# A hybrid attention and state-space decoder block: both value halves in one PSUM bank, another clock behind the order of all queues, and TensorE's order in attention taken from the source

## The chip, the core and the metric

The kernel runs on one core of one Trainium2 chip. The metric is the device time of one execution in microseconds (us); lower is better. The core has five engines with a queue each: TensorE (PE in the profile, its weight loads PEld), VectorE (DVE), ScalarE (ACT), GpSimd (POOL) and SyncE (SP, which here issues nearly all DMAs).

## What is computed

The reference is one decoder layer on x of 2048 tokens by 1024 channels, in float32. Cut to what matters here:

```
h = rmsnorm(x);  P = h @ W_in      # q, k, v, z_a, indexer q/k/w, z_b, x/B/C, dt, gates
A = attention(q, k, v) over the 256 keys that the indexer scores highest, 8 heads, 2 KV heads of 64
A = A * silu(z_a)
B = Mamba-2 scan (conv, 16 heads, chunks of 128), group norm with silu(z_b)
m = sigmoid(gA) * (A @ W_pa) + sigmoid(gB) * (B @ W_pb)
out = rmsnorm(x + m @ W_out)
```

## The kernel before

Products that need float32 accuracy are made of float16 halves: a value is split into a high half and a low half (the rest), and three products are added in PSUM. The tokens are 16 tiles of 128. The kernel runs in stages that overlap at their edges: the scan branch with its projections (to about 700 us of the profiled span), the indexer's scores, the search for the 256th score and the other projections (to about 1400), and attention together with the final products (from about 1400 to the end). Names below are those of the source.

**Attention.** For each query tile i (a block), `att_A(i)` loads q, splits it, transposes it by DMA into Q1, makes all scores once (L1398, tile `lq`) and lets VectorE take each row's maximum (L1401, `jk`, `mxs`). The maxima go as two extra columns into `q2t`, which a DMA transposes into Q2. `att_B(i)` then walks over the two KV heads g and the key tiles j <= i. One step makes the scores of four heads (L1495 with Q1, L1497 with Q2, tile `lg`), VectorE adds the mask (L1504), ScalarE takes the exponential (L1505) and its float16 high half `ph` (L1509), GpSimd the low half `pl` (L1512). The step's products with the values come three steps later (`LAG`), in `pv` for `ph` (L1431) and later still in `pv_lo` for `pl` (L1440). The value tile `Vt` holds, for each key, 64 high halves, a column of ones (it gives the sum of the exponentials) and 64 low halves: 129 columns. `pv` multiplies `ph` with all 129, `pv_lo` multiplies `pl` with the first 65. The result of two heads takes one PSUM bank, so four heads take two tiles of the pool `psO`, which has two: a group's first `pv` waits until the last group has been read out.

After a group's last step VectorE reads each bank out: reciprocal of the sums (L1447), copy of the high part (L1453), addition of the low part (L1454); GpSimd multiplies by the reciprocal (L1455). After both groups, `tail(i)` multiplies by silu(z_a) on VectorE (L1463, 128x512), and norm, split and a DMA transpose give `oT`.

**Final products.** `fin_M(i)` multiplies `oT` with W_pa (L1536 to L1538) and the scan's result with W_pb (L1543 to L1545), gates the two (L1548 to L1550), and splits and transposes into `mT`. `fin_O(i)` multiplies with W_out (L1574 to L1576) and adds x.

**What sets the order.** The source is a set of Python generators that `interleave` weaves: inside block i, the steps of `att_B(i)` are the main line, `att_A(i+1)` and the final products of earlier tiles are spread between them by fixed estimates. Block 0 and 1 and `att_A(2)` are woven with the last projections in `early_att`, ahead of `attention`. What is written in this order is then put in order once more when the program is built: a scheduler runs through a model of the machine, and whenever an engine is free by the model's clock, it takes for it the instruction written earliest among those whose inputs the model has ready. That fixes each engine's queue; the chip runs each queue strictly in that order. So an instruction that the model thinks late is overtaken by later ones, and one that it thinks ready stands where it is written, whatever the chip will find. In the profiled run TensorE's order from 750 to 1350 us is exactly that of the source; in the attention it departs from it by a few instructions here and by up to a hundred there; VectorE's departs from it everywhere.

Of the kernel before, what the change touches and what calls it, by code (L numbers as in the profile page):

```python
# [9 lines left out]
FT = mybir.dt.float32  # L10
# [5 lines left out]
AF = mybir.ActivationFunctionType  # L16
OP = mybir.AluOpType
# [4 lines left out]
P = 128  # L22
# [6 lines left out]
HD = 64  # L29
# [11 lines left out]
def MARK(label):  # L41
    pass


def _chain(*gens):
    for g in gens:
        yield from g


def _run_all(gen):  # L50
    while True:
        try:
            next(gen)
        except StopIteration as e:
            return e.value
# [10 lines left out]
def _pace(gen, t):  # L66

    while t > 0:
        try:
            w = next(gen)  # L70
        except StopIteration:
            return
        if w is None:
            return
        t -= w
        yield w
# [23 lines left out]
def interleave(main, sides):  # L100

    total = max(1e-9, main[1])
    done, pos = 0.0, [0.0] * len(sides)
    for w in main[0]:
        done += w
        for k, (gen, ln) in enumerate(sides):
            while pos[k] is not None and pos[k] < ln * done / total:
                try:
                    pos[k] += next(gen)
                except StopIteration:  # L110
                    pos[k] = None
    for k, (gen, ln) in enumerate(sides):
        if pos[k] is not None:
            for _ in gen:
                pass
# [32 lines left out]
XO = 0  # L148
# [9 lines left out]
def hybrid_block(ctx, tc, a, out, dbg=None):  # L158
    nc = tc.nc
    V, A, PL, PE, SP = nc.vector, nc.scalar, nc.gpsimd, nc.tensor, nc.sync  # L160

    def pool(name, bufs, **kw):
        return ctx.enter_context(tc.tile_pool(name=name, bufs=bufs, **kw))
# [510 lines left out]
    def scan(u):  # L674
# [89 lines left out]
        for k in range(4):  # L764
# [12 lines left out]
            elif u < 15:  # L777
                scan_load(u + 1, k - 2)
            yield 1
        TAIL.append(tail())  # L780

    def need(key):
# [357 lines left out]
    Vt = kv.tile([P, NT, G, 130], F16, name="Vt")  # L1140
# [178 lines left out]
    psO = pool("psO", 2, space=PSUM, reuse_waits="tile")  # L1319
# [10 lines left out]
    def rowscale(f2, name, pool_):  # L1330

        t = pool_.tile([P, 1], I32, name=name + "t", tag="rs1")
        s = pool_.tile([P, 1], I32, name=name + "s", tag=name + "s")
        v = pool_.tile([P, 1], I32, name=name + "v", tag=name + "v")
        V.tensor_scalar(t, f2.bitcast(I32), 1, 0x3F800000, OP.logical_shift_right, OP.bitwise_and)
        V.tensor_scalar(s, t, -1.0, 204.0 * 2 ** 23, OP.mult, OP.add)
        V.tensor_scalar(v, t, 50.0 * 2 ** 23, None, OP.add)
        return s.bitcast(FT), v.bitcast(FT)

    def split_T(src, s, t, dst, nb, pe=False):  # L1340

        A.activation(t[:, 0], src, AF.Copy, scale=s)
        n = nb * P // (2 if nb == KC else 1)
        for c in range(0, nb * P, n):
            V.scalar_tensor_tensor(t[:, 1, c:c + n], src[:, c:c + n], s, t[:, 0, c:c + n], OP.mult, OP.subtract)
        yield SPY
        if not pe:
            SP.dma_start_transpose(dst.rearrange("p a k t -> p (a k) t"), t.rearrange("p a n -> p (a n)"))
            return
        m = KC // nb  # L1350
        for hl in range(0, 2, m):
            pp = lgps2([P, m, nb, P], F16)
            for a in range(m):
                for k in range(nb):
                    PE.transpose(pp[:, a, k], t[:, hl + a, k * P:(k + 1) * P], id16)
            A.copy(dst[:, hl:hl + m], pp)
            yield KC * 0.056
# [4 lines left out]
    def load_mt(i):  # L1362

        mts[i] = at.tile([P, NT, P], BF, name="mkt")
        SP.dma_start_transpose(mts[i][:, 0:i + 1], msk[i, :, 0:(i + 1) * P])
# [56 lines left out]
    def pv():  # L1422

        MARK("attB")
        if len(plo) >= (PLD if lag > 1 else 1):
            pv_lo()
        i, g, j, ph, pl, B = pend.pop(0)
        if j == 0:
            B["po"] = [psO.tile([P, 2, 256], FT, name="po", tag="po") for _ in range(2)]
        for h in range(4):  # L1430
            PE.matmul(B["po"][h // 2][:, h % 2, 0:129], ph[:, h], Vt[:, j, g, 0:129], start=(j == 0 and h % 2 == 0), stop=False)  # L1431
        plo.append((i, g, j, pl, B))
        while j == i and plo:
            pv_lo()

    def pv_lo():
        i, g, j, pl, B = plo.pop(0)
        po, oa = B["po"], B["oa"]
        for h in range(4):
            PE.matmul(po[h // 2][:, h % 2, 0:65], pl[:, h], Vt[:, j, g, 0:65], start=False, stop=(j == i and h % 2 == 1))  # L1440
        if j == i:
            rc = at.tile([P, 4], FT, name="rc")
            for b in range(2):
                pob = po[b]
                oag = oa[:, 4 * g + 2 * b:4 * g + 2 * b + 2]
                rcb = rc[:, 2 * b:2 * b + 2]
                V.reciprocal(rcb, pob[:, :, 64])  # L1447
                if XO == 2:
                    for h in range(2):
                        A.activation(oag[:, h], pob[:, h, 0:64], AF.Copy, scale=rcb[:, h:h + 1])  # L1450
                        V.scalar_tensor_tensor(oag[:, h], pob[:, h, 65:129], rcb[:, h:h + 1], oag[:, h], OP.mult, OP.add)
                else:
                    V.tensor_copy(oag, pob[:, :, 0:64])  # L1453
                    V.tensor_tensor(oag, oag, pob[:, :, 65:129], OP.add)  # L1454
                    (V if XO else PL).tensor_tensor(oag, oag, rcb[:, :, None].to_broadcast([P, 2, HD]), OP.mult)  # L1455
            if g == G - 1:
                tails.append(tail(i, B))

    def tail(i, B):

        MARK("attB")
        oaf = B["oa"].rearrange("p h d -> p (h d)")
        V.tensor_tensor(oaf, oaf, B["za"].rearrange("p h d -> p (h d)"), OP.mult)  # L1463
        t = at.tile([P, 2, H * HD], F16, name="spa", bufs=1)
        f2 = at.tile([P, 1], FT, name="f2a")
        A.activation(t[:, 1].bitcast(BF), oaf, AF.Square, accum_out=f2)
        s_a, v_a = rowscale(f2, "ra", at)
        va = ac.tile([P, 1], FT, name="va", bufs=NQ)
        V.tensor_tensor(va, v_a, ra, OP.mult)
        oT = ac.tile([P, 2, 4, P], F16, name="oT", bufs=NQ)  # L1470
        yield
        yield from split_T(oaf, s_a, t, oT, 4, i == NT - 1)
        oTs[i] = (oT, va)

    def flush():
        while pend:
            pv()
        while tails:
            _run_all(tails.pop(0))
# [121 lines left out]
    def last(i):  # L1601
        if i == NT - 1:
            flush()
        return
        yield

    def fin_stream(first):
        for i in range(NT):
            o = fin_O(i - 1, fi) if i else iter(())
            while i not in oTs:  # L1610
                yield None
            if i == NT - 1:
                yield from _take(o, 8)
            mg_ = fin_M(i, fi)
            if i == 0:
                lw = load_out() if first else iter(())
                for w in mg_:
                    yield w
                    next(lw, None)
            elif i < NT - 1:  # L1620
                yield from _take(mg_, MO)
                yield from _zip(mg_, o, ZM, 16)
            else:
                yield from mg_
                yield from o
        yield from fin_O(NT - 1, fi)
# [27 lines left out]
    def attention(first):  # L1654
        nonlocal fi, at, pw, lag
        lag = LAG
        with tc.tile_pool(name="fi", bufs=2, reuse_waits="tile") as fi, tc.tile_pool(name="at", bufs=2, reuse_waits="tile") as at, \
                tc.tile_pool(name="pw", bufs=3, reuse_waits="tile") as pw:
            if not first:
                _run_all(att_A(0))  # L1660
            i0 = NA if first else 0
            if first:
                load_mt(NA)
            fs = fin_stream(first)
            wt = [max(tB(i), T_MIN) for i in range(NT)]
            rate = (NT - 1) * T_FIN / sum(wt[i0:])
            for i in range(i0, NT):
                sides = [(_pace(fs, rate * wt[i]), rate * wt[i])]
                if i + 1 < NT:
                    sides.append((att_A(i + 1), A_F * tA(i + 1)))  # L1670
                interleave((_chain(att_B(i), last(i)), tB(i)), sides)
            for _ in fs:
                pass

    attention(True)


    def exact_topk(gp):
# [95 lines left out]
```

## Time and profile before

| | |
|---|---|
| time, median of 3 runs | 2226.74 us (2224.58 to 2228.22) |
| profiled execution | 2230.14 us, span 2228.4 us |
| TensorE busy | 2037.3 us (91%), mean granted clock 0.973 of 2.4 GHz |
| VectorE busy | 1803.7 us (81%) |
| ScalarE, GpSimd busy | 1126.2 us (51%), 841.2 us (38%) |

The span is the time from the first to the last instruction; 1.7 us lie around it. A busy TensorE counts a matmul from its start to its modelled end, and matmuls overlap, so a pause shorter than that overlap doesn't show as idle.

### The profile page before, as it was taken

What the parts mean: (1) busy time and instruction counts of PE and PEld (TensorE: products, weight loads), DVE (VectorE), ACT (ScalarE), POOL (GpSimd) and SP (SyncE); (2) the same over time, 40 slices, a digit from 0 to 9 for tenths busy, and PEclk for the clock granted to TensorE, in tenths of its full rate; (3) what the DMA queues carried; (4) which work ended last, traced back from release to release, by engine and by line L of the source; (5) the groups of instructions that cost most, each with busy time, mean ns of one, the idle gap of its engine ahead of it and who ended that gap; (6) DMA issues with size and microseconds to landing.
All of it is one profiled execution on the core that took longest, in us unless ns stands there. A gap on an engine that the chain in (4) does not pass through costs nothing. (4 is left out here: it accounts for less than half of the span.)

```text
span 2228.4 us, 43416 instructions
## 1 busy us (share of the span) xinstructions
PE 2037.3 (91%) x15537; PEld 1386.7 (62%) x15537; DVE 1803.7 (81%) x4954; ACT 1126.2 (51%) x1971; POOL 841.2 (38%) x1208
## 2 busy tenths in 40 slices
PE   6889999899998999989999899988989899999997
PEld 5656666566766878768877788634444444544553
DVE  8888888988888567888998887577889888887763
ACT  5444443433342267646746731245566566666671
POOL 4423335533435433310102124124455444544550
PEclk9999999999999999999999999999999999999998
DMA  4444322322222332342344435485454334234231
GB/s 144 131 105 112 94 66 84 108 76 62 67 61 84 95 94 80 87 128 90 115 142 134 126 118 172 107 213 125 106 116 108 100 97 102 81 89 96 62 91 45
DMA packets 371195, 229.06 MB, mean 103 GB/s; under 512 B 209996, under 2 KB 333720, under 8 KB 370968
## 3 DMA queue, kind: packets, MB, share of 16 engines
q1 hardware_dynamic: 370968, 226.19, 37.9%
q8 instruction: 124, 2.03, 0.4%
q14 instruction: 103, 0.84, 0.1%
HBM read 123.82 MB, written 53.90 MB: 80 GB/s over the span
## 5 line engine op out<-in xcount | busy, mean ns | idle before, releaser
L1512 POOL TENSOR_TENSOR pl<-p,ph 128x512 f16<-128x512 f32 x272 | 328.3, 1211 | 428.8 <-ACT ph L1509 407.1
L1505 ACT ACTIVATE p<-p,lnb,qsc 128x512 f32<-128x512 f32 x270 | 217.3, 811 | 194.1 <-DVE p L1504 193.6
L443 PEld LDWEIGHTS <-xh 128*128 128x128 f16 x2560 | 250.6, 99 | 48.0 <-issue 12.8
L442 PEld LDWEIGHTS <-xh 128*128 128x128 f16 x2560 | 252.0, 99 | 41.2 <-issue 5.9
L444 PEld LDWEIGHTS <-xl 128*128 128x128 f16 x2560 | 250.7, 99 | 32.5 <-issue 2.5
L1504 DVE TENSOR_TENSOR p<-lg,mkt 128x512 f32<-128x512 f32 x266 | 181.2, 684 | 53.9 <-PE lg L1497 49.9
L1401 DVE CUSTOM_DVE_ANT_0 jk<-lq,mka 128x512 bf16<-128x512 f32 (+3 forms) x304 | 187.6, 617 | 33.9 <-PE lq L1398 27.7
L1509 ACT CAST ph<-p 128x512 f16<-128x512 f32 x272 | 165.3, 614 | 6.1
L1087 ACT ACTIVATE jkS<-sca,XX 128x384 int8<-128x384 f32 (+3 forms) x104 | 138.6, 1333 | 53.6 <-DVE XX L1077 34.9
L1398 PE MATMUL lq<-KK,Q 128*128 128x512 f16 (+3 forms) x320 | 103.2, 350 | 21.0 <-DVE mxs L1401 16.4
L1431 PE MATMUL po<-Vt,ph 128*128 128x129 f16 x1088 | 113.7, 221 | 8.8 <-DVE oa L1454 3.4
L1089 DVE TENSOR_SCALAR_CACHE_REDUCE jkV<-sca,XX 128x1536 uint8<-128x1536 f32 (+4 forms) x78 | 111.8, 1434 | 2.6
L1497 PE MATMUL lg<-Q,KK 128*128 128x512 f16 x272 | 102.9, 382 | 12.0 <-DMA Q<-q2t 12.0
L1495 PE MATMUL lg<-Q,KK 128*128 128x512 f16 x272 | 103.8, 382 | 6.8 <-DVE p L1504 6.7
L1166 ACT ACTIVATE gt<-gt 128x512 f32<-128x512 f32 x64 | 40.1, 627 | 135.6 <-DVE gt L1165 135.1
L1574 PE MATMUL fi<-wo,mT 128*128 128x512 f16 x256 | 98.4, 384 | 9.8 <-DMA mT<-spm 5.7
L951 ACT ACTIVATE r<-acc 128x512 f32<-128x512 f32 (+3 forms) x152 | 79.3, 542 | 49.3 <-DVE sca L952 32.4
L1440 PEld LDWEIGHTS <-pl 128*128 128x128 f16 x1088 | 66.3, 98 | 58.3 <-issue 5.7
L1543 PE MATMUL fi<-wpb,obt 128*128 128x512 f16 x256 | 97.6, 381 | 4.4 <-DVE gtl L1548 2.8
L1575 PE MATMUL fi<-wo,mT 128*128 128x512 f16 x256 | 98.7, 386 | 0.0
L1576 PE MATMUL fi<-wo,mT 128*128 128x512 f16 x256 | 98.6, 386 | 0.0
L1545 PE MATMUL fi<-wpb,obt 128*128 128x512 f16 x256 | 97.8, 382 | 0.0
(802 smaller groups left out, 6454.4 us busy)
## 6 DMA issues: line engine op xcount, KB each, us to landing
bc<-acr SPq DMA_DIRECT2D x64, 256.0 KB, 3.2
gd<-gt SPq DMA_DIRECT2D x64, 256.0 KB, 2.5
gtl<-gd SPq DMA_DIRECT2D x32, 512.0 KB, 4.4
xt<-in_x SPq DMA_DIRECT2D x16, 512.0 KB, 4.3
e<-ecr SPq DMA_DIRECT2D x128, 64.0 KB, 3.1
obn<-ohl SPq DMA_DIRECT2D x64, 128.0 KB, 2.2
pst<-in_w_out SPq DMA_DIRECT2D x16, 512.0 KB, 4.4
xr<-in_x SPq DMA_DIRECT2D x32, 256.0 KB, 3.1
```

Source lines behind the costliest of these rows:

```text
L442: PE.matmul(ps, xh[:, c, tk], hi[:, c], start=(first and c == 0), stop=False)
L443: PE.matmul(ps, xh[:, c, tk], lo[:, c], start=False, stop=False)
L444: PE.matmul(ps, xl[:, c, tk], hi[:, c], start=False, stop=(last and c == KC - 1))
L1087: A.activation(jkA[:, :n], sct[i], AF.Sign, bias=thr[:, 0, k:k + 1], scale=-1.0, accum_out=cnt[:, 0, k:k + 1])
L1089: V.tensor_scalar(jkV[:, :n], sct[i], thr[:, 0, k:k + 1], 0.0, OP.is_lt, OP.add, accum_out=cnt[:, 0, k:k + 1])
L1401: V.tensor_tensor_reduce(jk[:, :c1 - c0], ps[:, :c1 - c0], mk[:, c0:c1], 1.0, -BIG, OP.add, OP.max, mxs_[:, h, c:c + 1])
L1431: PE.matmul(B["po"][h // 2][:, h % 2, 0:129], ph[:, h], Vt[:, j, g, 0:129], start=(j == 0 and h % 2 == 0), stop=False)
L1495: PE.matmul(ps, KHt[g][:, js], Q1[:, hs], start=True, stop=False)
L1504: V.tensor_tensor(p32, ps, mb, OP.add)
L1505: A.activation(p32, p32 if masked and not onP else ps, AF.Exp, bias=lnb, scale=qsc[g])
L1509: A.copy(ph, p32)
L1512: PL.tensor_tensor(pl, p32, ph, OP.subtract)
```

## The change

Three things are changed. First, the four heads of a group share one PSUM bank of 4 x 128 floats: `ph` is multiplied with the 65 columns of high halves and ones and, in a second matmul, with the 64 low halves, which add onto the same 64 columns. What was left to VectorE after the group (copy, addition) is now done by the accumulation; one reciprocal and one multiplication straight from PSUM remain, and the multiplication with silu(z_a) goes to GpSimd, once for each group. Second, the scheduler's clock is another, more detailed model of the machine (`schedule_with_timeline_sim`), for the whole program. Third, TensorE's instructions in `attention` (blocks 2 to 15 and all final products) are not put in order by the scheduler; they keep the order of the source.

```
         if j == 0:
-            B["po"] = [psO.tile([P, 2, 256], FT, name="po", tag="po") for _ in range(2)]
+            B["po"] = psO.tile([P, 4, 128], FT, name="po", tag="po")
         for h in range(4):
-            PE.matmul(B["po"][h // 2][:, h % 2, 0:129], ph[:, h], Vt[:, j, g, 0:129], start=(j == 0 and h % 2 == 0), stop=False)
+            PE.matmul(B["po"][:, h, 0:65], ph[:, h], Vt[:, j, g, 0:65], start=(j == 0 and h == 0), stop=False)
+            PE.matmul(B["po"][:, h, 0:64], ph[:, h], Vt[:, j, g, 65:129], start=False, stop=False)
...
         for h in range(4):
-            PE.matmul(po[h // 2][:, h % 2, 0:65], pl[:, h], Vt[:, j, g, 0:65], start=False, stop=(j == i and h % 2 == 1))
+            PE.matmul(po[:, h, 0:65], pl[:, h], Vt[:, j, g, 0:65], start=False, stop=(j == i and h == 3))
         if j == i:
             rc = at.tile([P, 4], FT, name="rc")
-            for b in range(2):
-                pob = po[b]
-                oag = oa[:, 4 * g + 2 * b:4 * g + 2 * b + 2]
-                rcb = rc[:, 2 * b:2 * b + 2]
-                V.reciprocal(rcb, pob[:, :, 64])
...
-                    V.tensor_copy(oag, pob[:, :, 0:64])
-                    V.tensor_tensor(oag, oag, pob[:, :, 65:129], OP.add)
-                    (V if XO else PL).tensor_tensor(oag, oag, rcb[:, :, None].to_broadcast([P, 2, HD]), OP.mult)
+            oag = oa[:, 4 * g:4 * g + 4]
+            V.reciprocal(rc, po[:, :, 64])
+            V.tensor_tensor(oag, po[:, :, 0:64], rc[:, :, None].to_broadcast([P, 4, HD]), OP.mult)
+            PL.tensor_tensor(oag, oag, B["za"][:, 4 * g:4 * g + 4], OP.mult)
...
         oaf = B["oa"].rearrange("p h d -> p (h d)")
-        V.tensor_tensor(oaf, oaf, B["za"].rearrange("p h d -> p (h d)"), OP.mult)
...
-    attention(True)
+    with tc.manual_schedule(engines={PE.engine}):
+        attention(True)
...
-    with tile.TileContext(nc) as tc:
+    with tile.TileContext(nc, schedule_with_timeline_sim=True) as tc:
```

## Rows read from the trace of the kernel before

**Rows 1.** The page: busy time of each engine, its share of the span, its instructions.

```profile
PE 2037.3 (91%) x15537; PEld 1386.7 (62%) x15537; DVE 1803.7 (81%) x4954; ACT 1126.2 (51%) x1971; POOL 841.2 (38%) x1208
```

**Rows 2.** Busy time in stretches: PE, PEld, DVE, ACT, POOL, granted clock, DMA.

```profile
0.00:1400.00 1400.00, 1290.96 (x10319) 994.32 (x10320) 1158.03 (x3233) 658.58 (x1211) 485.12 (x872) 0.97 0.36 103
...
1480.00:2229.00 749.00, 677.33 (x4724) 349.79 (x4722) 596.31 (x1563) 438.31 (x712) 337.35 (x314) 0.98 0.39 95
...
500.00:600.00 100.00, 99.59 (x666) 69.36 (x664) 84.37 (x214) 39.72 (x88) 40.03 (x58) 1.00 0.22 63
900.00:1000.00 100.00, 87.27 (x713) 71.59 (x712) 87.16 (x260) 55.40 (x104) 23.64 (x69) 0.93 0.41 112
```

**Rows 3.** TensorE's waits from 1400 us on: total us, times, longest.

```profile
PE lq L1398 <- DVE mxs L1401: 16.4, 27, 1.8
PE lg L1497 <- DMA Q<-q2t: 12.0, 9, 2.8
PE lg L1495 <- DVE p L1504: 6.7, 8, 2.0
...
PE po L1431 <- DVE oa L1454: 3.4, 7, 1.1
PE fi L1536 <- DVE gtl L1549: 3.3, 2, 1.8
PE fi L1574 <- DVE gtl L1548: 2.9, 2, 1.9
PE fi L1543 <- DVE gtl L1548: 2.8, 1, 2.8
...
PE po L1431 <- DVE rc L1447: 1.4, 1, 1.4
```

**Rows 4.** TensorE's waits before 1400 us: two small helper products.

```profile
PE trp L257 <- ACT jkS L251: 11.8, 3, 7.2
...
PE trp L992 <- DVE w_branch_ac L986: 4.9, 1, 4.9
```

**Rows 5.** TensorE's timeline: start, length (from first start to last end), line, count.

```profile
1975.25 0.39 PE L1431 MATMUL po<-Vt,ph 128*128 128x129 f16 x4
1975.47 0.38 PE L1574 MATMUL fi<-wo,mT 128*128 128x512 f16 x1
...
2143.29 0.41 PE L1440 MATMUL po<-Vt,pl 128*128 128x65 f16 x8
2143.53 0.38 PE L1536 MATMUL fi<-wpa,oT 128*128 128x512 f16 x1
```

**Rows 6.** Groups by line: count, busy us, mean ns; a weight load, the read-out, its nearest relatives.

```profile
L1440 PEld LDWEIGHTS <-pl 128*128 128x128 f16 x1088 | 66.3, 98 | 58.3 <-issue 5.7
...
L1447 DVE RECIPROCAL rc<-po 128x2 f32<-128x2 f32 x64 | 10.3, 160 | 9.6 <-PE po L1440 9.1 <-POOL oa L1455 0.5
L1454 DVE TENSOR_TENSOR oa<-oa,po 128x128 f32<-128x128 f32 x64 | 18.1, 283 | 0.5
L1453 DVE COPY oa<-po 128x128 f32<-128x128 f32 x64 | 17.7, 277 | 0.0
L1463 DVE TENSOR_TENSOR oa<-oa,za 128x512 f32<-128x512 f32 x16 | 16.3, 1021 | 8.0 <-POOL oa L1455 8.0
L704 DVE TENSOR_TENSOR xd<-trp,dts 128x256 f32<-128x256 f32 x64 | 26.5, 416 | 5.1 <-ACT xk L702 4.6
...
L1455 POOL TENSOR_TENSOR oa<-oa,rc 128x128 f32<-128x128 f32 x64 | 29.2, 463 | 19.4 <-DVE oa L1454 18.2
L734 POOL TENSOR_TENSOR zu<-xk,zu 128x256 f32<-128x256 f32 x64 | 53.5, 836 | 97.1 <-DVE xk L733 90.6 <-DVE hz L572 4.5 <-DVE ss L431 1.7
```

**Rows 7.** TensorE's timeline at the start of block 2.

```profile
1443.97 0.32 PE L1398 MATMUL lq<-KK,Q 128*128 128x384 f16 x1
1444.13 0.38 PE L1545 MATMUL fi<-wpb,obt 128*128 128x512 f16 x1
...
1450.65 0.59 PE L1497 MATMUL lg<-Q,KK 128*128 128x512 f16 x2 [0.96 <-DMA Q<-q2t]
```

## Prediction before the run

> **What bounds the kernel now.** I read the page first: TensorE is busy for 91% of the span, VectorE for 81% [rows 1]. Either could be the bound, so the stretches come next. Before 1400 us TensorE is busy for 1291.0 of 1400 us, from 1480 us on for 677.3 of 749 us, and VectorE for 596.3 of the same 749 [rows 2]. TensorE leads in both, with 109 us idle in the first and 72 us in the second, and VectorE is close behind in attention. The reader is to see also how far two stretches lie apart: TensorE is 99.6% busy at the full clock from 500 to 600 us, 87.3% busy at 0.93 of it from 900 to 1000. So there is something to win from the order alone, about 12 us in 100 at the worst place.
>
> Then the waits, which say who keeps TensorE idle. In attention VectorE is named most: the maxima (16.4), the mask (6.7) and the gating (3.3, 2.9, 2.8) make 32.1 us, the read-out of the value products 3.4 + 1.4 = 4.8 us; the transposed Q2 is named for 12.0 us in nine waits [rows 3]. Before attention some are of another kind: TensorE stands still for 11.8 and 4.9 us ahead of one-column helper products, whose input is late, though the projections written behind them need nothing of it [rows 4]. Such a wait is a matter of order alone.
>
> **The split of the value product.** 272 steps times 4 heads give 1088 matmuls of 129 columns, which become 2176 of 65 and 64. Four of 129 columns start at 1975.25 and the next matmul at 1975.47: 55 ns each. Eight of 65 columns in a row run from 2143.29 to 2143.53: 30 ns each [rows 5]. So 2 x 30 - 55 = 5 ns more for each of 1088: +5 us. It can't be a gain, so the lower bound is 0. The upper bound is that each added weight load is paid in full: 98 ns [rows 6] times 1088 = 107 us. I take the low end, because the eight in a row have a weight load each and yet start 30 ns apart, so loads are hidden at just this shape. The Trainium skill says otherwise (TensorE: Matmul & The Clock Gate, section Back-to-back issue gap): pairs of weight load and matmul are sustained at about 81 ns at 128 columns. By that the two halves would take 162 in place of 55 ns, an estimate of +116 us. Those two sentences are for the rival below; no term uses them.
>
> **The read-out.** Per group VectorE now does two reciprocals (160 ns), two copies (277) and two additions (283), 1.44 us, and per block the product with z_a (1021): 64 x 0.72 + 16 x 1.02 = 62.4 us [rows 6]. After it there is one reciprocal (not shown with four columns; with two 160, and I take that) and one product of 128x256 from PSUM with a broadcast; its exact relative is L704, 416 ns [rows 6]. 32 x 0.576 = 18.4 us, so VectorE loses 44 us of work. GpSimd drops 64 x 0.463 = 29.6 us and gains 32 products of 128x256 at L734's 836 ns = 26.8 us [rows 6]; I cost that at nothing, since GpSimd is busy for 337 of 749 us [rows 2] and the chain from a block's last value product to its norm gets shorter, 2 x 0.72 x 2 + 0.46 + 1.02 = 4.4 us at most against 0.16 + 0.42 + 0.84 = 1.4 (only the second group's part of it lies on the chain, so 2.9 against 1.4). Without GpSimd's slack, the `pl` of the next step would be late by 0.84 us per group, and the value products behind it: 27 us. `za` is needed one group earlier than before, but its load is written at the block's head, a whole group of steps ahead, so nothing waits for it.
>
> A group now holds one bank of the pool of two, so the next group's first value product finds a free bank: the 4.8 us of waits for the read-out go [rows 3]. I take -4; bounds -5 and 0. The other 32.1 us name VectorE for other work. If the 44 us come out just where TensorE waits, all 32 go; if they come out where VectorE idles anyway (153 of 749 us [rows 2]), none. The work removed sits at the group ends alone, while the waits for maxima and mask are spread over 27 and 8 places, so I take a quarter: -8.
>
> **TensorE in attention as written.** Now, where the model thinks an input late, later work overtakes. Block 2 shows it: its last maxima product starts at 1443.97, Q2 arrives and the first L1497 starts at 1450.65, 6.7 us later; final products fill this up to 0.96 us [rows 7]. In the source L1497 stands right behind its L1495 at the head of the block, and what is written behind it must now wait: `pv`, the next maxima, the final products; who waits in turn is VectorE's mask and the whole chain to `ph`. The profile's nine waits for Q2 are at the first steps of blocks 0 to 8; blocks 2 to 8 lie in the part now ordered by the source, so seven stalls. At worst each costs the 6.7 us of block 2, 47 us. At best the maxima products, no longer overtaken either, finish so much earlier that the 12.0 us go: -12. From block 3 on the maxima are written to end before the block does (`A_F` spreads them 1.2 times as densely), so I am nearer to the low end: today's wait of 12.0/9 = 1.3 us comes once more at seven places, +9.
>
> **The clock of the order.** The trace can't show an order that has not been. From above, 109 us of idle time before attention [rows 2] is all there is to win. From below, I use the two stretches: if three of the full ones fall to the state of 900 to 1000, that is 3 x 12.3 = +37 us. A model that sees the helper products' inputs late puts projections ahead of them: 11.8 + 4.9 = 16.7 us [rows 4]. The smaller waits, some 90 us, are for the scan's and the accumulators' chains, and I give a tenth of them: 8. Together -25. For VectorE's queue in attention, which also gets another order, I take 0; what speaks for a gain is in the quarter above.
>
> **Sum.** 2230.1 + 5 - 4 - 8 + 9 - 25 = 2207 us against the profiled execution. That one is 3.4 us over the median of 2226.7, so the forecast is 2204 us, 1.0% faster.
>
> **Rivals.**
> Source order stalls TensorE (the other side). TensorE's queue has one head; with the order fixed, each late Q2 is paid. At the upper end of that term the sum is 2230.1 + 5 - 4 - 8 + 47 - 25 - 3.4 = 2242 us. It decides from 32 us on, 4.6 us at each of seven blocks. For it: block 2 alone had 6.7 us to fill. Against it: from block 9 on no wait for Q2 is among the nine, and the blocks concerned are the short ones. Chance 0.22.
> The other clock orders the first 1400 us worse: +37 in place of -25 gives 2266 us. For it: today's order yields 99.6% from 500 to 600 us, which can only get worse there. Against it: 87.3% from 900 to 1000. Chance 0.10.
> Both orders clear most waits: half of the 109 us and all of the 32.1 go: 2230.1 + 5 - 4 - 32 - 54 + 9 - 3.4 = 2151 us. For it: each pause also costs clock (0.93 in the worse stretch). Against it: chains of the scan don't get shorter by order. Chance 0.15.
> The change doesn't do what it says: the new clock leaves the queues nearly as they are, and VectorE's 44 us come out where it idles: 2230.1 + 5 - 4 - 3.4 = 2228 us. For it: TensorE's order is that of the source for long stretches already. Chance 0.09.
> Weight loads are exposed by twelve short matmuls in a row: 2204 - 5 + 107 = 2306 us. Against it: the eight in a row [rows 5]. Chance 0.03. The rule of the Trainium skill quoted above is this rival; so far the trace contradicts it (30 against 81 ns).
>
> **How the numbers follow.** My forecast has 0.41 and, by its terms, reaches from 2170 (all of VectorE's 32 us, -35 for the clock) to 2222. The range from 2148 to 2258 leaves out half of the double gain (0.07), most of the worse first part (0.07) and the weight loads (0.03). What this kernel's measurement tells from no change is about 0.2%, 4.5 us. Faster: 0.41 + 0.15 + 0.02 from the low end of the stalls = 0.58. Within 0.2%: 0.10, nearly all from the fourth rival. Slower: the rest, 0.32.
>
> **What would show it.** In the profile of the changed kernel: value products of 65 and 64 columns 30 ns apart (right) or near 100 (wrong). L1453, L1454 and L1463 gone, VectorE's busy time some 44 us lower from 1400 us on, and no wait of a value product for the read-out. L1497's waits for Q2: near 20 us in all if I am right, near 50 if the first rival is. TensorE idle before attention near 85 us instead of 109, with the wait of L257 gone; if it is over 130 the second rival holds. I am wrong altogether if TensorE's waits in attention move to another name, the transposed `mT` above all, which source order also puts at the head of the queue.

## The result and the profile after

The changed kernel takes 2277.57 us (median of 5 runs, 2272.99 to 2280.62); the kernel before took 2228.22 us beside it. The ratio is 1.0219 with a 95% interval of 1.0203 to 1.0234: 2.2% slower, 49 us. The forecast was 2204 us with a range up to 2258; it missed in sign and range. The medians of the kernel before in the experiments' runs lie between 2229.57 and 2230.43, and the 95% intervals of the ratios are 2.5 to 8 us wide to either side; so differences of medians below are good to a few us, and one of 5 us says little.

The page of the changed kernel, its busy line, answers to [rows 1]:

```profile
span 2275.5 us, 45400 instructions
PE 2050.6 (90%) x16625; PEld 1397.9 (61%) x16625; DVE 1770.5 (78%) x4810; ACT 1129.9 (50%) x1971; POOL 818.8 (36%) x1176
```

VectorE has lost 33 us of busy time and the span has grown all the same. Where, the busy time by stretch tells (PE, PEld, DVE, ACT, POOL, then granted clock, DMA share, GB/s), as in [rows 2]:

```profile
0.00:1400.00 1400.00, 1311.04 (x10581) 1016.93 (x10582) 1158.61 (x3284) 666.28 (x1224) 474.82 (x876) 0.98 0.38 105
1400.00:1480.00 80.00, 52.37 (x326) 24.68 (x324) 39.53 (x95) 26.46 (x45) 18.71 (x17) 0.83 0.64 175
1480.00:2276.00 796.00, 687.21 (x5723) 356.27 (x5720) 572.39 (x1431) 437.16 (x704) 325.28 (x283) 0.96 0.35 86
```

The first 1400 us hold 20 us more of TensorE's work than before. All is lost after that: 109 us idle from 1480 us on, where it was 72, and only 52 of the 80 us busy in the stretch in which blocks 2 and 3 begin (first Q2 products at 1418.7 and 1459.2 us). The first Q2 product of block 0 starts at 1384.9 us (before: 1404.8), 20 us early; the end comes 47 us late. So attention takes 67 us more, and the part ahead of it 20 us less.

Who keeps TensorE idle from 1400 us on (total, times, longest), beside [rows 3]:

```profile
PE lq L1398 <- DVE mxs L1401: 50.5, 65, 3.6
PE lg L1488 <- DMA Q<-q2t: 18.9, 4, 6.8
PE fi L1565 <- DMA mT<-spm: 11.2, 4, 4.1
PE fi L1534 <- DVE gtl L1539: 9.7, 8, 3.3
PE lq L1398 <- DMA Q<-q: 5.3, 1, 5.3
PE lg L1486 <- DVE p L1495: 4.7, 6, 1.6
PE lg L1355 <- ACT spm L1342: 4.1, 1, 4.1
PE po L1441 <- POOL pl L1503: 3.9, 6, 1.2
```

The wait for the read-out is gone; the scores' wait for the mask has fallen from 6.7 to 4.7 us. The maxima's wait has tripled, from 16.4 to 50.5 us, and it comes 65 times.

What such a wait looks like, in TensorE's timeline (start, duration, engine, line, what, then idle time before it and its releaser):

```profile
1439.04 1.03 PE L1398 MATMUL lq<-KK,Q 128*128 128x512 f16 x2 [5.32 <-DMA Q<-q]
...
1440.81 0.63 PE L1486 MATMUL lg<-Q,KK 128*128 128x512 f16 x1
1441.24 0.63 PE L1488 MATMUL lg<-Q,KK 128*128 128x512 f16 x1
...
1442.82 0.38 PE L1536 MATMUL fi<-wpb,obt 128*128 128x512 f16 x1
1443.04 0.38 PE L1534 MATMUL fi<-wpb,obt 128*128 128x512 f16 x1
...
1445.41 0.38 PE L1536 MATMUL fi<-wpb,obt 128*128 128x512 f16 x1
1445.63 0.59 PE L1398 MATMUL lq<-KK,Q 128*128 128x512 f16 x2
1446.80 0.38 PE L1398 MATMUL lq<-KK,Q 128*128 128x512 f16 x1 [0.57 <-DVE mxs L1401]
1447.64 0.38 PE L1398 MATMUL lq<-KK,Q 128*128 128x512 f16 x1 [0.47 <-DVE mxs L1401]
1447.85 0.38 PE L1486 MATMUL lg<-Q,KK 128*128 128x512 f16 x1
```

Fifteen final products run in one piece from 1442.12 to 1445.63. Then four maxima products come in one piece. Each fills one PSUM bank of the pool `psQ`, which has two, and VectorE must have read a bank before it is filled again. So the first two start at once, the third and the fourth wait at the head of TensorE's queue, and the scores behind them wait too. VectorE over the same time:

```profile
1446.04 0.69 DVE L1401 CUSTOM_DVE_ANT_0 jk<-lq,mka 128x512 bf16<-128x512 f32 x1 [2.77 <-PE lq L1398]
1446.66 0.08 DVE L1401 DVE_READ_ACCUMULATOR2_ANT mxs<- 128x1 f32 x1
1446.89 0.69 DVE L1401 CUSTOM_DVE_ANT_0 jk<-lq,mka 128x512 bf16<-128x512 f32 x1
```

It sat idle for 2.77 us while the final products ran. Then it needs 0.85 us for each maximum, where TensorE makes such a product in 0.22 us, and TensorE waits. The two engines take turns at waiting. In the kernel before, the final products lie between the maxima products (TensorE's timeline in block 3, where the maxima of block 4 are made):

```profile
1493.77 0.38 PE L1398 MATMUL lq<-KK,Q 128*128 128x512 f16 x1
1493.98 0.38 PE L1575 MATMUL fi<-wo,mT 128*128 128x512 f16 x1
1494.20 0.38 PE L1576 MATMUL fi<-wo,mT 128*128 128x512 f16 x1
1494.42 0.38 PE L1536 MATMUL fi<-wpa,oT 128*128 128x512 f16 x1
1494.63 0.22 PE L1398 MATMUL lq<-KK,Q 128*128 128x128 f16 x1
```

The source writes the clump. In `interleave`, each main step lets the first side stream (the final products) catch up fully, then the second (`att_A` with its maxima products). The scheduler took the clump apart, and `manual_schedule` stops it from doing so. A count over both traces from 1400 to 2200 us shows it: maxima products come three to six in a row, with no other product between them, 31 times in the changed kernel and twice in the kernel before. The 65 waits are more than these runs, since pairs that follow each other closely also find no free bank.

### The profile page after: what moved, and what is told of

Its sections match the earlier page's. It is cut to its first block, busy times and chain, and to the rows that moved or that the text cites. A ratio compares the mean times of both kernels' runs of the same rounds, so it can differ in the third digit from the quotient of the medians.

```text
span 2275.5 us, 45400 instructions
## 1 busy us (share of the span) xinstructions
PE 2050.6 (90%) x16625; PEld 1397.9 (61%) x16625; DVE 1770.5 (78%) x4810; ACT 1129.9 (50%) x1971; POOL 818.8 (36%) x1176
## 4 chain that ended last, share of the span: by engine, by line
PE 42%; DVE 30%; DMA 11%; issue 8%; ACT 6%; SPq 2%; POOL 2%; DVEq 0%; POOLq 0%; ACTq 0%
PE acc L442 3%; PE acc L444 3%; PE acc L443 3%; DVE jk L1401 3%; ACT jkS L1087 2%; DVE cac L549 2%; PE fi L1534 2%; PE fi L1535 2%; PE fi L1536 2%; DVE bc L699 2%; PE fi L1565 2%; PE lq L1398 2%; PE fi L1567 2%; PE fi L1566 2%; PE lg L1486 2%
## 5 line engine op out<-in xcount | busy, mean ns | idle before, releaser
L1398 PE MATMUL lq<-KK,Q 128*128 128x512 f16 (+3 forms) x320 | 96.8, 351 | 56.3 <-DVE mxs L1401 50.5
L1488 PE MATMUL lg<-Q,KK 128*128 128x512 f16 x272 | 105.0, 387 | 19.0 <-DMA Q<-q2t 18.9
L1565 PE MATMUL fi<-wo,mT 128*128 128x512 f16 x256 | 101.5, 396 | 18.4 <-DMA mT<-spm 11.2
L1534 PE MATMUL fi<-wpb,obt 128*128 128x512 f16 x256 | 99.3, 388 | 10.3 <-DVE gtl L1539 9.7
L1431 PE MATMUL po<-Vt,ph 128*128 128x65 f16 x1088 | 105.2, 194 | 3.6 <-ACT ph L1500 3.6
L1432 PE MATMUL po<-Vt,ph 128*128 128x64 f16 x1088 | 105.7, 196 | 0.0
L699 DVE TENSOR_SCALAR bc<-bc,acm 128x128 f32<-128x128 f32 x256 | 93.8, 424 | 11.4 <-DMA bc<-acr 11.1
L1566 PE MATMUL fi<-wo,mT 128*128 128x512 f16 x256 | 101.2, 395 | 0.0
L1567 PE MATMUL fi<-wo,mT 128*128 128x512 f16 x256 | 100.7, 393 | 0.3 <-ACT mT L1356 0.3
```

Of the source, the lines that this page charges most:

```text
L1565: PE.matmul(pq, mT[:, 0, k], wout[0][:, k, cs_], start=(k == 0), stop=False)
L1566: PE.matmul(pq, mT[:, 0, k], wout[1][:, k, cs_], start=False, stop=False)
```

## The experiments

All compute the whole output. The theories' letters are those of the expectations.

**One part each.** e1_bank has only the bank and the split; e2_clock only `TileContext(nc, schedule_with_timeline_sim=True)`; e3_source only this:

```diff
-    attention(True)
+    with tc.manual_schedule(engines={PE.engine}):
+        attention(True)
```

> The bank and the split alone, clock and TensorE's order as before. Theory S (TensorE held to the source order costs the time, the other parts gain a little): 2215 to 2232 us, 44 us less VectorE work in attention, TensorE's waits for the read-out gone. Rival B (the split or the single bank costs it): 2245 us or more. Rival C (the new clock's order of the other queues costs it): as theory S.

> The new clock alone, for all queues, TensorE's in attention too; value halves in two banks as before. Theory S: the 20 to 30 us that the start of attention came earlier in the changed kernel are kept, 2195 to 2212 us. Rival C (the clock's order of VectorE, ScalarE and SyncE spoils attention whatever TensorE's order): start of attention as early, but 2250 us or more. Rival B: 2195 to 2212 us.

> TensorE in attention as written alone, the clock of before, two banks. Theory S: attention is longer by 60 to 80 us, 2285 to 2310 us, TensorE's waits for the maxima 45 us or more. Rival C: within 10 us of the kernel before, since the old clock orders the other queues. Rival B: as rival C.

Measured: e1_bank 2219.61 us, ratio 0.9963 (0.9951 to 0.9976), -8 us by the ratio and -10 by the medians: as forecast. e2_clock 2239.34, 1.0043 (1.0030 to 1.0057), +10: all three theories missed. e3_source 2308.24, 1.0359 (1.0340 to 1.0379), +79: theory S in the time, though its waits for the maxima, 42.6 us, stay under the 45 that S named. TensorE's largest waits from 1400 us on in e3_source:

```profile
PE lq L1398 <- DVE mxs L1401: 42.6, 64, 1.9
PE lg L1497 <- DMA Q<-q2t: 19.3, 6, 6.2
PE po L1431 <- DVE oa L1454: 15.3, 18, 1.9
```

So the loss is the order taken from the source, it is far above the upper bound of that term (+47), and Q2 is not its largest wait. The read-out's wait, 3.4 us in [rows 3], becomes 15.3 here; it is the one that the bank takes away in the changed kernel.

**Two parts each.** e4_bank_clock is the changed kernel without the diff above; e5_bank_source is the changed kernel with `TileContext(nc)`; e6_clock_source is the changed kernel with the value tile, the products and the read-out of before.

> The changed kernel without the source order: bank and clock, TensorE ordered by the new clock. Theory S: 2190 to 2210 us, faster than before by 20 to 35 us, waits for the maxima back to some 15 us. Rival C: 2250 us or more. Rival B: 2240 us or more.

> Bank and source order, old clock. If the parts add (bank -8, source order +80): 2290 to 2302 us. If the single bank relieves the source order of its waits for the read-out (15.3 us with source order alone, 4.8 before): 2280 to 2290 us.

> New clock and source order, two banks. Theory P (the new clock brings attention 15 to 27 us earlier, and what it loses alone it loses in attention by letting final products run ahead, which the source order forbids): 2278 to 2292 us, well under the 2308 of the source order alone. Rival A (the parts add, the clock costs 10 us wherever it stands): 2312 us or more.

Measured: e4_bank_clock 2227.42 us, 0.9989 (0.9978 to 1.0000); the 2190 to 2210 of S fails, and so do the higher times of B and C. e5_bank_source 2290.11, 1.0269 (1.0242 to 1.0296), on the border of its two expectations, so it settles neither. e6_clock_source 2289.63, 1.0257 (1.0231 to 1.0284): P, and A falls. The source order costs 2290.1 - 2219.6 = 70.5 us on top of the bank, 2289.6 - 2239.3 = 50 on top of the clock, and 2277.6 - 2227.4 = 50 on top of both. The clock costs 10 us alone, yet with the source order it wins 2308.2 - 2289.6 = 19 us. With the bank it wins 2290.1 - 2277.6 = 12.5 us there. The parts don't add up: what the clock spoils in attention, the fixed order of TensorE takes back in large part.

**The clump itself.** e7_alternate is the changed kernel with the two side streams taken in turn, one piece of each:

```diff
...
+        more = True
+        while more:
+            more = False
+            for k, (gen, ln) in enumerate(sides):
+                if pos[k] is not None and pos[k] < ln * done / total:
+                    more = True
+                    try:
+                        pos[k] += next(gen)
...
-                interleave((_chain(att_B(i), last(i)), tB(i)), sides)
+                interleave2((_chain(att_B(i), last(i)), tB(i)), sides)
```

> The changed kernel, with the side streams of attention written in turn: one product of the maxima, one triple of final products, and so on, where the source has all final products of a step and then all its maxima products. Same instructions, same clock, same three parts. Theory K (the source order loses because maxima products written one behind the other wait at the head of TensorE's queue for VectorE to free one of two banks): waits for the maxima from 50 us to under 20, 2240 to 2256 us. Rival L (it loses by the long chains to Q2, mT and the gating at the head of the queue): 2268 to 2282 us, the waits moved to other names.

Measured: 2241.95 us, 1.0060 (1.0039 to 1.0081), 36 us under the changed kernel: K. The waits of the maxima:

```profile
PE lq L1420 <- DVE mxs L1423: 23.4, 35, 2.4
```

They fall from 50.5 to 23.4 us, not under 20 as K said. The work is the same, only the two streams are woven finer (and the other engines' queues are ordered anew from that source). Runs of three or more maxima products are left 3 times, where there were 31, and the waits for Q2 (18.8 us) and `mT` (15.6 us) don't fall: the clump is what went.

**The two banks.** The bank saved by the change can be given to the maxima. e12_one_value_bank is the control, the changed kernel with one bank for the values; e11_three_score_banks adds the third bank:

```diff
-    psO = pool("psO", 2, space=PSUM, reuse_waits="tile")
+    psO = pool("psO", 1, space=PSUM, reuse_waits="tile")
...
-PQ_ = 2
+PQ_ = 3
```

(`PQ_` only in e11_three_score_banks, where the sizes of the pools `psS` and `psF` are kept.)

> The changed kernel with three PSUM banks for the maxima products in place of two, the third taken from the value products (one in place of two). Theory K: waits for the maxima fall from 50 us to under 25, and the time is 15 to 30 us under that of the run with one value bank alone. Rival L: no more than 5 us under it.

> The changed kernel with one PSUM bank for the value products in place of two, and nothing else: the control for the run before. A group's first value product waits for the read-out of the last group, a reciprocal and one multiplication, some 0.6 us at 28 places: 2280 to 2298 us.

Measured: e11_three_score_banks 2243.08 us, 1.0055 (1.0036 to 1.0074); e12_one_value_bank 2272.63, 1.0189 (1.0171 to 1.0208). The third bank wins 29.5 us against its control: K. The maxima's waits, first in the control, then with three banks:

```profile
PE lq L1398 <- DVE mxs L1401: 44.8, 60, 2.7
PE po L1431 <- DVE oa L1446: 1.6, 3, 1.0
```

```profile
PE lg L1488 <- DMA Q<-q2t: 23.4, 5, 11.0
PE lq L1398 <- DVE mxs L1401: 12.9, 24, 1.4
```

With the source's order of TensorE untouched (runs of three or more come 32 times here), one more buffer takes 32 of 44.8 us away. That is a second remedy, of another kind, with the same effect: it is the bank that the clump waits for. The expectation for the control missed: a single value bank costs nothing, since its wait for the read-out is 1.6 us.

**The clock, stage by stage.** e8_clock_first_part is e1_bank with the new clock for everything written ahead of `attention` (blocks 0 and 1 are among it) and the old one, with the scheduler's order, in `attention`. e9_first_part_alternate adds `interleave2` to it.

```diff
+    blk = tc.block(schedule_with_timeline_sim=True)
+    blk.__enter__()
     x_d = a["x"][0]
...
+    blk.__exit__(None, None, None)
     attention(True)
```

> One bank; the new clock orders only the part before attention, as a section of the program that all engines leave together; the old clock orders attention, TensorE too. Theory P: the first part ends some 15 to 20 us earlier as under the new clock, attention lasts as with the bank alone: 2200 to 2210 us. Rival M (what the new clock wins in the first part is work moved across the border, and the border itself costs): 2218 us or more.

> The new clock for the first part and the old one for attention, one bank, and attention's side streams written in turn. Theory K: under the old clock the scheduler already moves maxima products out of each other's way (14 us of waits for the maxima), so writing them in turn gains little: 2194 to 2204 us. Rival N (writing them in turn helps whatever the order): 2185 us or less.

Measured: e8_clock_first_part 2201.59 us, 0.9870 (0.9846 to 0.9895): P, faster than both kernels by 1.3% and 3.3%. e9_first_part_alternate 2200.05, 0.9849 (0.9811 to 0.9886): K, the weaving adds nothing where a scheduler already undoes the clump. So the clock wins 2219.6 - 2201.6 = 18 us ahead of `attention` (12 us of it are there when the first Q2 product starts, at 1387.6 us against 1399.7 in e1_bank), and in `attention` it costs 2227.4 - 2201.6 = 26 us when it also orders TensorE.

What it does there is seen in the counts of one kind of final product (the first matmul of `fin_O`, L1574: TensorE's busy time and number in two stretches), first before, then in e2_clock:

```profile
1440.00:1640.00 200.00, 19.80 (x53) 5.17 (x53) 0.97 0.64 153
1840.00:2040.00 200.00, 24.26 (x64) 6.25 (x64) 0.99 0.39 94
```

```profile
1440.00:1640.00 200.00, 30.35 (x80) 7.81 (x80) 0.97 0.57 134
1840.00:2040.00 200.00, 18.46 (x49) 4.79 (x49) 0.93 0.35 80
```

Under the new clock 80 in place of 53 are done early and 49 in place of 64 late, where all of e2_clock's instructions fill less of TensorE's time than before (the same stretch, all engines; first before, then e2_clock):

```profile
1840.00:2040.00 200.00, 188.89 (x1360) 99.19 (x1358) 168.23 (x450) 128.46 (x205) 99.61 (x90) 0.99 0.39 94
```

```profile
1840.00:2040.00 200.00, 170.53 (x1248) 88.74 (x1246) 157.79 (x426) 124.74 (x197) 96.52 (x90) 0.93 0.35 80
```

The pair that gives the 26 us shows the same: e4_bank_clock does 80 early and 48 late, e8_clock_first_part 59 and 64. The final products are the filler of attention; spent early, they are missing later. That this is the cause of the 26 us is argued from these rows and not shown; no run changed the filler alone. One rival is that the new model thinks Q2 ready too early: TensorE's waits for it are 23.5 us in e4_bank_clock and 10.9 in e8_clock_first_part, the largest difference between the two lists.

**Where the source order still costs.** e7_alternate is 40 us above e8_clock_first_part. e10_source_middle is e7_alternate with TensorE's order fixed only in blocks 5 to 14, so that the scheduler orders the short first blocks and the last one:

```diff
+                if first and i == 5:
+                    held.enter_context(tc.manual_schedule(engines={PE.engine}))
+                if first and i == NT - 1:
+                    held.close()
...
-    with tc.manual_schedule(engines={PE.engine}):
-        attention(True)
+    attention(True)
```

> The changed kernel with side streams written in turn, and TensorE held to the source order only in blocks 5 to 14; blocks 2 to 4 and the last one are ordered by the new clock. Theory Q (what the source order still costs after the streams alternate, some 40 us, is paid in the short first blocks and in the last, by the chains to Q1, Q2 and mT): 2210 to 2225 us. Rival R (it is paid all along): 2234 to 2242 us.

Measured: 2219.18 us, 0.9939 (0.9916 to 0.9961): Q, 23 us under e7_alternate. TensorE over the start of attention (busy, matmuls, clock, DMA share, GB/s), in e7_alternate and in e10_source_middle:

```profile
1380.00:1480.00 100.00, 70.31 (x518) 0.85 0.61 160
```

```profile
1380.00:1480.00 100.00, 92.65 (x704) 0.97 0.70 185
```

The same 100 us take 704 matmuls in place of 518. In e7_alternate TensorE stands in this stretch for 9.4 us at Q2 products, 8.0 us for q and 6.5 us for `mT`, each at the head of a queue that may not be overtaken; in e10_source_middle it stands for 5.5 us at a Q2 product and 0.9 us for q. Over the whole of attention Q2's waits are equal (18.8 and 19.0 us), so these 23 us go with q and other late inputs more than with Q2. The last block was not tried apart. The remaining 2219.2 - 2201.6 = 18 us are open: the fixed order in blocks 5 to 14, or the new clock in the other engines' queues.

## Why the prediction was wrong

**The split (+5) and the bank (-4, -8) were right in sum.** Together -7 forecast, -8 measured in e1_bank (-10 by the medians). Apart they were not measured: in the trace of e1_bank the read-out's 4.8 us of waits are gone, and those for the maxima and the mask are 1.6 and 3.0 us shorter. The halves run as foreseen (TensorE's timeline in the changed kernel):

```profile
2002.57 0.28 PE L1441 MATMUL po<-Vt,pl 128*128 128x65 f16 x4
2002.69 0.19 PE L1431 MATMUL po<-Vt,ph 128*128 128x65 f16 x1
2002.72 0.20 PE L1432 MATMUL po<-Vt,ph 128*128 128x64 f16 x1
...
2002.91 0.19 PE L1432 MATMUL po<-Vt,ph 128*128 128x64 f16 x1
2002.94 0.38 PE L1398 MATMUL lq<-KK,Q 128*128 128x512 f16 x1
```

Twelve short products with a weight load each, the eight halves in 0.25 us: 31 ns each, as in [rows 5]. The rival of exposed weight loads falls. The Trainium skill (TensorE: Matmul & The Clock Gate, section Back-to-back issue gap) gives about 81 ns for such pairs at 128 columns. The traces here disagree: 31 ns at 64 and 65 columns, and 55 ns at 129 columns in [rows 5], in pieces of eight and four. The read-out's new instructions were priced well (VectorE and GpSimd groups from 1400 us on; durations after the bar):

```profile
L1446 DVE TENSOR_TENSOR oa<-po,rc 128x256 f32<-128x256 f32 x30 | 12.7, 422 | 0.6
L1445 DVE RECIPROCAL rc<-po 128x4 f32<-128x4 f32 x30 | 5.1, 171 | 0.3 <-PE po L1441 0.3
```

```profile
L1447 POOL TENSOR_TENSOR oa<-oa,za 128x256 f32<-128x256 f32 x30 | 22.3, 744 | 34.7 <-DVE oa L1446 19.7 <-issue 8.2 <-DVE f2m L1543 1.8
```

422, 171 and 744 ns against 416, 160 and 836 forecast. VectorE's busy time fell by 33 us, not 44. The durations of the read-out's instructions fell as forecast, from 62.4 to 19.0 us over the whole run; busy time counts a moment in which two instructions overlap once, so it need not fall by as much. One other group also grew: the gating's last addition (L1541, before L1550) takes 36.5 us in place of 27.4 (28.1 in e1_bank).

**"TensorE in attention as written" (+9, bounds -12 and +47) is the step that failed.** It measured +70.5 on top of the bank under the old clock (e5_bank_source against e1_bank), which is the case that it forecast; +79 alone and +50 on top of both other parts. The step asked one question, what is written behind a late Q2 product, and priced seven such stalls at 21 us in all, 12 of them there before. That price was about right: 18.9 us in four waits, the first of them block 2's, as long as the 6.7 us that the prediction read there:

```profile
1418.67 0.58 PE L1488 MATMUL lg<-Q,KK 128*128 128x512 f16 x1 [6.76 <-DMA Q<-q2t]
```

What it never asked is how the source spaces the products that share a small pool. The scheduler did two jobs, it overtook late inputs and it broke clumps, and only the first was in the sum. The clump's cost was found by e7_alternate (-36 us) and e11_three_score_banks (-29.5 us). The two remedy one thing and are not added. Blocks 2 to 4 and 15 hold 23 us more (e10_source_middle against e7_alternate). At the start of attention the waits there are of the kind foreseen, one head and a late input, but for q and `mT` as well as Q2.

The prediction's own test would have misled: it named Q2's waits near 20 us as the sign of being right, and they are 18.9 us. It did say that a move of the waits to another name would be the sign of being wrong; the name was the maxima, not mainly `mT` (11.2 us).

**The clock: -25 in the first part, 0 in attention.** The first is -18 measured (e8_clock_first_part against e1_bank), too large by 7 us but right in sign and mechanism: TensorE idles 89 us before 1400, where 85 were forecast. The named helper waits nearly went: L257's for `jkS` fell from 11.8 to 0.4 us, and the largest at that line is now 3.4 us for another input; L992's fell from 4.9 to 2.1 us (waits ahead of 1400 us in the changed kernel; the first is the largest left):

```profile
PE lgp L721 <- DVE xk L733: 10.7, 9, 2.2
...
PE trp L257 <- ACT z3lo L251: 3.4, 1, 3.4
...
PE trp L992 <- DVE w_branch_ac L986: 2.1, 1, 2.1
```

The 0 for attention was meant for VectorE's queue, since in the changed kernel the new clock doesn't order TensorE there. With the source's order in place the clock wins 12.5 us in all (e5_bank_source against the changed kernel). The first Q2 product starts 24 us earlier (1384.9 against 1409.0 us), and 18 us were won ahead of `attention` by the other pair, so by one or the other 6 to 11 us are lost in attention. That is little beside an uncertainty of 7 us: the 0 was not far off, but no bound was given for it. The 26 us (e4_bank_clock against e8_clock_first_part) arise only where the new clock orders TensorE too, and are no error of the sum.

**The rivals.** The first one, that source order stalls TensorE, had the right sign and place but 2242 us, since it was priced by Q2 alone; 2278 lies beyond all that it allowed for. The worse first part, the double gain, the idle change and the weight loads all fall.

**The sum by the runs.** In the prediction's terms, by medians: bank and split -10 where it had -7, the source's order +70.5 where it had +9, the new clock on top of both -12.5 where it had -25. Such differences along one chain of kernels add up to the measured +48 whatever the cause, so the sum proves nothing; it shows which term was wrong, by 61 of the 71 us. Another chain, with the clock before the source's order, reads -10, -18, +26 and +50: what a part costs depends on the others beside it.

## What to carry to other kernels

Before an order is fixed by hand, list for every pool with few buffers the longest run of its producers in the written order: beyond the number of buffers each costs a consumer's time at the head of the queue. A scheduler hides such clumps, so price its removal by everything that it moved, not by the one overtaking that the trace names. Try a change of the scheduler's model stage by stage: here the same switch was worth -18 us in one stage and, where it ordered TensorE too, +26 in the next.

## What the runs showed that was not expected

After its wait of 5.32 us at 1439.04 TensorE is slow for a while: matmuls of 512 columns start 0.43 us apart (1440.81 to 1441.24, the 1.2 GHz level) and from 1442.82 on 0.22 us apart (2.4 GHz). The same follows the wait of 6.76 us ahead of 1418.67 (0.43 us apart up to 1421.6). These pauses are so paid a second time: the granted clock from 1400 to 1480 us is 0.83 in the changed kernel.

One PSUM bank for the values costs nothing against two (2272.63 and 2277.57 us), though the products of the next group must wait for the read-out: with the shorter read-out that wait is 1.6 us in all in e12_one_value_bank, and 4.8 us in e11_three_score_banks.
